# A decoder layer whose dense products are multiplied by Strassen's algorithm instead of block by block

## The chip, the cores and the metric

The kernel runs on one core of one Trainium2 chip. The metric is the device time of one execution in microseconds (us). The kernel before took 1522.94 us (median of 3 runs, 1522.55 to 1523.62).

## The reference

One layer on 1024 tokens of width 1024, in float32: an RMS norm, one wide projection whose columns feed two branches (a gated MLP with spatial mixing, and a Mamba-2 scan, SSD), their outputs projected and merged, and two more dense products at the end.

```python
h = rms_norm(x, norm_g)
u, v, z_a, z_b, xbc, dt_raw, g_a, g_b = split(h @ w_in)        # 1024 x 10272
o_a = gmlp_branch(u, v, z_a, ...) @ w_oa                       # 1024 x 1024
xbc = silu(causal_depthwise_conv(xbc, conv_w, conv_b))         # xs 2048, B 512, C 512 columns
y   = ssd_scan(xs, softplus(dt_raw + dt_bias), a_log, B, C, d_skip)
o_b = gated_group_rms_norm(y, z_b, ssm_norm_g) @ w_ob          # 2048 x 1024
x   = x + (sigmoid(g_a) * o_a + sigmoid(g_b) * o_b) @ w_out    # 1024 x 1024
x   = x + sigmoid(rms_norm(x, ple_norm_g) @ w_pg) * (p @ w_ple)
return rms_norm(x, final_g)
```

## The kernel before, in words

To keep float32 accuracy, both operands of a product are split into two float32r parts, hi (a rounded copy) and lo (the rest), and three products are summed: hi·hi, hi·lo, lo·hi. `mm3` (L89) issues them; every dense matmul has line L97, but those of v (L515). Splitting costs one copy (ScalarE, L228 or L112) and one subtraction (GpSimd L229 for weights of the projections, VectorE L113, L573 elsewhere).

The normed and transposed h stays on chip as `hhi`, `hlo`, 8 k-tiles by two halves of 512 tokens. `in_proj` (L237) loads 128 columns of `w_in`, splits them and makes 48 matmuls of 512 columns (8 k-tiles, 2 halves, 3 parts) into two PSUM banks. From there each stage reads: `conv_tile` (L332) does the convolution on VectorE straight from PSUM (L339), `ssd_chunk` (L352) is the scan of 128 tokens of one of four groups, `z_tile` and `group_out` gate and norm, `gate_tile` writes the tanh of the gates to DRAM. Phase 2 (gMLP) makes v with 768 matmuls of 256 columns, mixes, and projects z_a and u. Phase 3 multiplies `w_ob`, `w_oa` in six parts of 512 rows, adding into tiles `m`; phase 4 multiplies `w_out` (`px`) and `w_pg` (`ppg`). The small product p·w_ple stands at the very start, while x is loaded.

An automatic scheduler sets the order of instructions on each engine from the written program. Loads are on SP's queue, most loads of intermediate results on POOL's; each queue and each engine works in order.

Of the kernel before, what the change touches and what calls it, by code (L numbers as in the profile page):

```python
# [24 lines left out]
O_U, O_V, O_ZA, O_ZB, O_XS, O_B, O_C, O_DT, O_GA, O_GB = (  # L25
    0, 1024, 2048, 3072, 5120, 7168, 7680, 8192, 8224, 9248)


@with_exitstack
def kernel(  # L30
# [38 lines left out]
    tri = const.tile([P, P], F32, name="tri")  # L69
    nc.gpsimd.memset(tri, 1.0)  # L70
    nc.gpsimd.affine_select(out=tri, in_=tri, pattern=[[1, P]], compare_op=ALU.is_ge,
                            fill=0.0, base=0, channel_multiplier=-1)
    triq = const.tile([P, P], F32, name="triq")
    nc.gpsimd.tensor_scalar(out=triq, in0=tri, scalar1=0.25, scalar2=None, op0=ALU.mult)
    # sel[k, m] = 1 in the last row
    sel = const.tile([P, P], F32, name="sel")
    nc.gpsimd.memset(sel, 1.0)
    nc.gpsimd.affine_select(out=sel, in_=sel, pattern=[[0, P]], compare_op=ALU.is_ge,
                            fill=0.0, base=-(P - 1), channel_multiplier=1)
# [8 lines left out]

    def mm3(pst, ahi, alo, bhi, blo, first, last, hh=(0, 1)):  # L89
        # pst[h] += (ahi + alo)^T (bhi + blo), for each half h of b's columns  # L90
        seq = [(ahi, b, h) for h in hh for b in (bhi, blo)] + [(alo, bhi, h) for h in hh]
        seen = set()
        cnt = {0: 0, 1: 0}
        for a, b, h in seq:
            cnt[h] += 1
            o_ = pst[h] if isinstance(pst, list) else pst[:, h, :]
            nc.tensor.matmul(o_, lhsT=a, rhs=b[h],  # L97
                             start=(first and h not in seen), stop=(last and cnt[h] == 3))
            seen.add(h)

    # ------------------------------------------------------------ p w_ple, kept for the end
    hsl = [slice(0, 512), slice(512, 1024)]

    def two(t):
        return [t[:, hsl[0]], t[:, hsl[1]]]

    def load_rows(name, src, row, a, b):
        # a, b: the destinations of the two parts, as halves
        raw = wp.tile([P, 1024], F32, tag="raw", name=f"raw_{name}")
        nc.sync.dma_start(out=raw, in_=src[row:row + P, :])  # L110
        for h in range(2):
            nc.scalar.copy(out=a[h], in_=raw[:, hsl[h]])  # L112
            tt(out=b[h], in0=raw[:, hsl[h]], in1=a[h].bitcast(F32), op=ALU.subtract)  # L113
        return a, b

    def w_slots(name):
        return (two(wp.tile([P, 1024], F32R, tag="whi", name=f"hi_{name}")),
                two(wp.tile([P, 1024], F32R, tag="wlo", name=f"lo_{name}")))

    def big_slots(name):  # L120
        return (two(big.tile([P, 1024], F32R, tag="big", name=f"hi_{name}")),
                two(big.tile([P, 1024], F32R, tag="big", name=f"lo_{name}")))

    ppd = dram.tile([S, D], F32, name="ppd")
    pts = [big.tile([P, NCH // 2, 256], F32, tag="big", name=f"ptm{i}") for i in range(2)]
    p_v = p.rearrange("(t q) e -> q t e", q=P)
    for i in range(2):
        nc.sync.dma_start(out=pts[i], in_=p_v[:, 4 * i:4 * i + 4, :])
        if i == 0:
            wple = [load_rows(f"wple{k}", w_ple, k * P, *w_slots(f"wple{k}")) for k in range(2)]  # L130
    # ------------------------------------------------------------ phase 0: h = rms_norm(x), transposed
    ss0 = const.tile([P, NCH], F32, name="ss0")
    rstd0 = const.tile([P, NCH], F32, name="rstd0")
    xt = []
    for t in range(NCH):
        xv = big.tile([P, D], F32, tag="big", name=f"x0_{t}")
        nc.sync.dma_start(out=xv, in_=x[t * P:(t + 1) * P, :])
        xt.append(xv)

    # per-column vectors, as columns  # L140
    n_cv = 4 * 24
    vrow2 = t2.tile([72, P], F32, tag="hst", name="vrow2")
    o = 0
    offs = {}
    for nm, ap_, n in (("ng", norm_g, 8), ("sg", ssm_norm_g, 16), ("cb", conv_b, 24),
                       ("lg", ln_a_g, 8), ("lb", ln_a_b, 8)):
        nc.scalar.dma_start(out=vrow2[o:o + n, :], in_=ap_.rearrange("(t q) -> t q", q=P))
        offs[nm] = o
        o += n
# [12 lines left out]

    phi = [two(big.tile([P, S], F32R, tag="big", name=f"phi{k}")) for k in range(2)]
    plo = [two(big.tile([P, S], F32R, tag="big", name=f"plo{k}")) for k in range(2)]
    for i in range(2):
        for k in range(2):
            pt = ps_ss(f"ptp{k}_{i}")
            for c in range(4):
                nc.tensor.transpose(out=pt[:, c * P:(c + 1) * P], in_=pts[i][:, c, k * P:(k + 1) * P],
                                    identity=ident)  # L170
            nc.vector.tensor_copy(out=phi[k][i], in_=pt)
            tt(out=plo[k][i], in0=pt, in1=phi[k][i].bitcast(F32), op=ALU.subtract)
# [5 lines left out]
    def halves(dt, tag, name):  # L178
        return [hp_.tile([P, 512], dt, tag=tag, name=f"{name}_{h}") for h in range(2)]

    hhi = [halves(F32R, "hA", f"hhi{k}") for k in range(KD)]
    hlo = [halves(F32R, "hB", f"hlo{k}") for k in range(KD)]
    for hf in range(2):
        h4 = slice(4 * hf, 4 * hf + 4)
        for t in range(4 * hf, 4 * hf + 4):
            junk = t4.tile([P, D], F32, tag="t4", name=f"sq0_{t}")
            act(junk, xt[t], AF.Square, accum_out=ss0[:, t:t + 1])
        rms_rstd(rstd0[:, h4], ss0[:, h4], eps1, 1.0 / D)
        for t in range(4 * hf, 4 * hf + 4):
            ts(out=xt[t], in0=xt[t], scalar1=rstd0[:, t:t + 1], scalar2=None, op0=ALU.mult)  # L190
        if hf == 0:
            pv = ps_ss("pv")
            nc.tensor.transpose(out=pv[:, 128:128 + NV2], in_=vrow2[:NV2, :], identity=ident[:NV2, :NV2])
            nc.tensor.transpose(out=pv[:, 0:n_cv], in_=vrow1, identity=ident[:n_cv, :n_cv])
            nc.vector.tensor_copy(out=vT, in_=pv[:, 128:128 + NV2])
            nc.vector.tensor_copy(out=cwT, in_=pv[:, 0:n_cv])
        for k in range(KD):
            pt = ps_ss(f"pt0_{hf}_{k}")
            for i in range(4):
                nc.tensor.transpose(out=pt[:, i * P:(i + 1) * P],  # L200
                                    in_=xt[4 * hf + i][:, k * P:(k + 1) * P], identity=ident)
# [150 lines left out]
    def ssd_chunk(g, c, xs, bT, cT, hst):  # L352
# [63 lines left out]
        if last:  # L416
            return None
# [309 lines left out]
```

## Time and profile before

| | |
|---|---|
| median of 3 runs | 1522.94 us |
| span of the profiled execution | 1521.2 us (1.7 us under the median) |
| TensorE (PE) busy | 1495.8 us, 98% |
| VectorE (DVE), ScalarE (ACT), GpSimd (POOL) busy | 694.6, 582.8, 524.2 us |
| bytes moved by DMA | 163.62 MB, mean 108 GB/s |

The span runs from the first to the last instruction. The chain of work that ended last is followed back from the end; what stands on it sets the time. A busy share of another engine matters only where TensorE waits for it.

### The profile page before, as it was taken

How to read it: one execution, taken by the hardware profiler on the slowest of the kernel's cores; microseconds unless marked ns; L12 is line 12 of the kernel's file. 1: busy time of each engine (PE TensorE's matmuls, PEld its weight loads, DVE VectorE, ACT ScalarE, POOL GpSimd, SP SyncE). 2: the span in 40 equal slices, each digit the busy share in tenths (PEclk: the TensorE clock that was granted, in tenths of full speed). 3: DMA queues.
4: the chain of work that ended last, by engine and by line, in shares of the span. 5: the costliest groups of instructions: out<-in, count | busy, mean ns of one | idle time of the engine just before them, and what ended most of it. 6: DMA issues, size and time to landing. Idle time of an engine off the chain costs nothing.

```text
span 1521.2 us, 18888 instructions
## 1 busy us (share of the span) xinstructions
PE 1495.8 (98%) x7628; PEld 1248.1 (82%) x7628; DVE 694.6 (46%) x1012; ACT 582.8 (38%) x924; POOL 524.2 (34%) x446
## 2 busy tenths in 40 slices
PE   6999999999999999999999999999999999999997
PEld 5788888878888888889999988888888888888885
DVE  5554477557656764430000432333133567831554
ACT  6453565555556545442112211122322111421454
POOL 1223656465557645651222211222322233100110
PEclk9999999999999999999999999999999999999999
DMA  8321222322142232342221221223332345534541
GB/s 277 104 73 56 84 70 64 117 83 70 56 125 76 64 112 83 117 152 71 84 83 56 77 77 56 69 85 116 125 111 97 135 170 186 189 125 150 215 186 56
DMA packets 124763, 163.62 MB, mean 108 GB/s; under 512 B 6292, under 2 KB 97636, under 8 KB 124676
## 3 DMA queue, kind: packets, MB, share of 16 engines
q1 hardware_dynamic: 107984, 102.90, 21.4%
q0 software_dynamic: 16464, 59.43, 11.4%
q8 instruction: 60, 0.98, 0.3%
q14 instruction: 27, 0.22, 0.0%
q10 hardware_dynamic: 228, 0.08, 0.0%
HBM read 128.71 MB, written 33.69 MB: 107 GB/s over the span
## 4 chain that ended last, share of the span: by engine, by line
PE 92%; issue 2%; DVE 2%; ACT 1%; DMA 1%; POOL 1%; SPq 0%; DVEq 0%; ACTq 0%; POOLq 0%
PE po L97 16%; PE ps_xs L97 11%; PE ps_zb L97 9%; PE psv L515 6%; PE ps_ga L97 6%; PE ps_za L97 6%; PE ps_gb L97 6%; PE px L97 6%; PE ps_u L97 6%; PE ppg L97 5%; PE ps_C L97 3%; PE ps_B L97 2%; PE pyo L406 2%; PE pyd L401 2%; PE psv L544 1%
## 5 line engine op out<-in xcount | busy, mean ns | idle before, releaser
L97 PE MATMUL po<-yh,whi_o 128*128 128x512 f32 x384 | 149.5, 389 | 0.5 <-DVE gt L603 0.5
L97 PE MATMUL po<-yl,whi_o 128*128 128x512 f32 x384 | 149.4, 389 | 0.0
L97 PE MATMUL po<-yh,wlo_o 128*128 128x512 f32 x384 | 118.2, 389 | 0.0
L97 PE MATMUL ps_zb<-hhi,whi_zb 128*128 128x512 f32 x256 | 101.9, 398 | 0.0
L97 PE MATMUL ps_zb<-hlo,whi_zb 128*128 128x512 f32 x256 | 101.3, 396 | 0.0
L97 PE MATMUL ps_xs<-hhi,whi_xs 128*128 128x512 f32 x256 | 100.4, 392 | 0.0
L97 PE MATMUL ps_xs<-hlo,whi_xs 128*128 128x512 f32 x256 | 100.0, 391 | 0.0
L229 POOL TENSOR_TENSOR wlo_o<-raw_o,whi_o 128x1024 fp32r<-128x1024 f32 x24 | 57.8, 2407 | 103.5 <-ACT whi_o L228 103.5
L97 PEld LDWEIGHTS po<-yh,whi_o 128*128 128x128 f32 x384 | 72.1, 188 | 15.9 <-issue 0.9
L97 PEld LDWEIGHTS po<-yh,wlo_o 128*128 128x128 f32 x384 | 72.1, 188 | 14.9
L97 PEld LDWEIGHTS po<-yl,whi_o 128*128 128x128 f32 x384 | 72.0, 188 | 14.9
L414 POOL TENSOR_TENSOR cv_xs<-cv_xs,ex 128x128 f32<-128x128 f32 x112 | 72.3, 672 | 34.1 <-DVE ex L409 34.0
L394 ACT ACTIVATE lm<-lm,cs 128x128 f32<-128x128 f32 x256 | 78.6, 389 | 12.3 <-DMA lm<-csd 11.8
L339 DVE SCALAR_TENSOR_TENSOR cv_xs<-ps_xs,cwT,cv_xs 128x1023 f32<-128x1023 f32 (+2 forms) x48 | 61.5, 1281 | 43.0 <-ACT cv_xs L336 42.0
L97 PE MATMUL ps_zb<-hhi,wlo_zb 128*128 128x512 f32 x256 | 80.7, 394 | 0.0
L97 PE MATMUL ps_xs<-hhi,wlo_xs 128*128 128x512 f32 x256 | 79.8, 393 | 0.0
L528 DVE BATCH_NORM_STATS2 bst<-v 128x6 f32<-128x128 f32 x64 | 13.2, 278 | 141.2 <-ACT v L518 141.2
L228 ACT CAST whi_o<-raw_o 128x1024 fp32r<-128x1024 f32 x24 | 25.3, 1052 | 133.7 <-PE po L97 99.9
L515 PE MATMUL psv<-whi_v,hhi 128*128 128x256 f32 x256 | 72.9, 285 | 0.0
L392 ACT ACTIVATE ex<-lm 64x512 f32<-64x512 f32 x56 | 35.3, 631 | 97.8 <-DMA lm<-csd 82.8
L515 PE MATMUL psv<-whi_v,hlo 128*128 128x256 f32 x256 | 72.4, 283 | 0.0
L515 PE MATMUL psv<-wlo_v,hhi 128*128 128x256 f32 x256 | 72.4, 283 | 0.0
(289 smaller groups left out, 3833.6 us busy)
## 6 DMA issues: line engine op xcount, KB each, us to landing
lm<-csd POOLq DMA_DIRECT2D x32, 512.0 KB, 4.3
raw_xs<-in_w_in_dram SPq DMA_DIRECT2D x16, 512.0 KB, 4.6
raw_zb<-in_w_in_dram SPq DMA_DIRECT2D x16, 512.0 KB, 3.8
ybd<-cv_xs SPq DMA_DIRECT2D x16, 512.0 KB, 5.2
yraw<-ybd POOLq DMA_DIRECT2D x16, 512.0 KB, 3.8
raw_o<-in_w_ob_dram SPq DMA_DIRECT2D x16, 512.0 KB, 3.4
gt<-tad POOLq DMA_DIRECT2D x16, 512.0 KB, 4.3
x<-in_x_dram SPq DMA_DIRECT2D x8, 512.0 KB, 8.7
```

The lines of the kernel that those rows point to most:

```text
L97: nc.tensor.matmul(o_, lhsT=a, rhs=b[h], start=(first and h not in seen), stop=(last and cnt[h] == 3))
L228: nc.scalar.copy(out=whi[:, :n], in_=raw[:, :n])
L229: nc.gpsimd.tensor_tensor(out=wlo[:, :n], in0=raw[:, :n], in1=whi[:, :n].bitcast(F32), op=ALU.subtract)
L339: stt(out=a[:, sh:], in0=ps[:, :S - sh], scalar=cw(k, ci), in1=a[:, sh:], op0=ALU.mult, op1=ALU.add)
L392: act(ex[h * HD:(h + 1) * HD], lv[h * HD:(h + 1) * HD, :, h, :], AF.Exp)
L394: act(lm[:, r_, :], lm[:, r_, :], AF.Relu, bias=cs[:, c, g * HG + r_:g * HG + r_ + 1], scale=-1.0)
L401: nc.tensor.matmul(pyd[h * HD:(h + 1) * HD, (r_ // 2) * P:(r_ // 2 + 1) * P], lhsT=xdt[:, r_, :], rhs=lm[:, r_, :], start=True, stop=True)
L406: nc.tensor.matmul(pyo[:, j * P:(j + 1) * P], lhsT=hst[:, 2 * j:2 * j + 2, :].rearrange("s r d -> s (r d)"), rhs=cT[:, cl], start=True, st ...
L414: nc.gpsimd.tensor_tensor(out=xs[j][:, cl], in0=xs[j][:, cl], in1=ex[:, j, :], op=ALU.add)
L515: nc.tensor.matmul(pf[:, i, :], lhsT=a[hf][:, i * P:(i + 1) * P], rhs=w_[:, k % 4, :], start=(k == 0 and n_ == 0), stop=(k == KD - 1 and n ...
L528: nc.vector.bn_stats(out=bst[:, c, j, :], in_=v[j][:, c, :])
L544: nc.tensor.matmul(psv[:, i * P:(i + 1) * P], lhsT=v[j][:, 4 * hf + i, :], rhs=wsT[:, g, :], start=True, stop=True)
```

## The change

All dense products but dt's (1024 x 1024 times 1024 x 32) and p·w_ple become multiplications of one form, `gemm`: the left operand gives 256 columns (two tiles of 128), the right operand is 1024 x 1024; both are cut in half along the inner dimension too, so there are 2 x 2 blocks on each side and four result blocks of 128 x 512. Strassen's algorithm in Winograd's form needs seven block products (of 4 k-tiles by 3 parts, 12 matmuls) where the plain way has eight. There are 60 such multiplications, of 84 matmuls of 512 columns.

- The left side (`a_side`): four additions on VectorE make S1 to S4, and seven pieces are split (ACT copy, POOL subtraction, L146), for each multiplication. Buffers: three raw tiles (a multiplication takes two), four hi and four lo pieces of seven.
- The right side: seven combinations (B11, B21, B22, T1 to T4) of 4 k-tiles, split, 56 tiles that stay on chip. For h they are made at the start (`h_sums`). For the five later products (two halves of `w_ob`, `w_oa`, `w_out`, `w_pg`) `sums_b` forms them early and writes them to DRAM, and `load_b` reads and splits them into the same 56 slots (8 more for one combination), each free when the last multiplication of the product before has used it.
- Between products PSUM is copied out three times (`snap`, ACT), and each result block is the sum of a bank and a copy (`mat`, VectorE).
- Since results come as halves of two tiles, stages meet through DRAM: conv's output `xbd`, the scan's `yd`, gated `ybd`, v, sums of the output products `md`. Loads and stores go to SP's queue. The scan's three products a chunk with xs are one instruction each now (POOL L622, L630, VectorE L631); convolution reads a float32 tile on chip (L494, L497), no longer PSUM. p·w_ple moves between `w_oa` and `w_out`.
- Order: convolution and v first, then the 32 scan chunks spread over 20 multiplications, then gMLP and gates, then the output products.

```diff
-    def in_proj(name, col):
-        whi, wlo = w_cols(name, col)
-        ps = ps_mm(f"ps_{name}")
-        for k in range(KD):
-            mm3(ps, whi[:, k, :], wlo[:, k, :], hhi[k], hlo[k], k == 0, k == KD - 1)
-        return flat(ps)
...
+        def split(nm, raw, lo_on):
+            hi = wpl.tile([P, 4, P], F32R, tag="wh", name=f"{nm}h_{name}", bufs=4)
+            lo = wpl.tile([P, 4, P], F32R, tag="wl", name=f"{nm}l_{name}", bufs=4)
+            nc.scalar.copy(out=hi, in_=raw)
+            lo_on(out=lo, in0=raw, in1=hi.bitcast(F32), op=ALU.subtract)
+            return hi, lo
+        res = {}
+        res["B11"] = split("a11", a11, ptt)
+        res["B21"] = split("a12", a12, ptt)
+        s1 = sm("s1")
+        tt(out=s1, in0=a21, in1=a22, op=ALU.add)
+        s2 = sm("s2")
+        tt(out=s2, in0=s1, in1=a11, op=ALU.subtract)
+        res["T2"] = split("s2", s2, ptt)
+        res["T1"] = split("s1", s1, ptt)
...
+    def gemm(name, loads, B, epi):
+        A = a_side(name, loads)
+        def prod(pst, c, first):
+            for k in range(4):
+                mm3(pst, (A[c][0][:, k, :], A[c][1][:, k, :]), B[c][k], first and k == 0, k == 3, True)
...
+        xb = ps_mm(f"x_{name}")
+        prod(xb, "B11", True)
+        u1 = snap("u1", xb)
+        ab = ps_mm(f"a_{name}")
+        prod(ab, "B21", True)
+        epi(0, 0, ab, u1)
+        prod(xb, "T2", False)
+        u2 = snap("u2", xb)
+        cb = ps_mm(f"c_{name}")
+        prod(cb, "T1", True)
+        prod(xb, "T3", False)
+        u3 = snap("u3", xb)
+        epi(1, 1, cb, u3)
+        db = ps_mm(f"d_{name}")
+        prod(db, "T4", True)
+        epi(1, 0, db, u3)
+        prod(cb, "B22", False)
+        epi(0, 1, cb, u2)
...
+                dma(out=t, in_=src)
+                res[c].append(split_b(f"{nm}_{c}_{k}", t, ("ap", "av", "vp", "av")[k], c == "B22"))
```

In `split_b` the first letter names the engine of the copy (a: ACT, v: DVE), the second that of the subtraction (v: DVE, p: POOL).

Three places of the order on the engines. First POOL inside the scan of group 0, before: one chunk and the start of the next (`wlo_xs`: lo part of the next convolution's weights, 1024 columns; `hst`, `dx`, `dxl`: the scan's state; `cv_xs`: its output).

```order
L414 TENSOR_TENSOR cv_xs_0_787<-cv_xs_0_787,ex_4_1262 128x128
L414 TENSOR_TENSOR cv_xs_1_850<-cv_xs_1_850,ex_4_1262 128x128
L414 TENSOR_TENSOR cv_xs_2_913<-cv_xs_2_913,ex_4_1262 128x128
L414 TENSOR_TENSOR cv_xs_3_976<-cv_xs_3_976,ex_4_1262 128x128
L229 TENSOR_TENSOR wlo_xs_1_1911<-raw_xs_1_1909,whi_xs_1_1910 128x1024
L427 TENSOR_TENSOR hst_5_1369<-hst_4_1302,cdec 128x512
L379 TENSOR_TENSOR dx_5_1323<-xdt_5_1321,dec_502 128x512
L386 TENSOR_TENSOR dxl_5_1326<-dx_5_1323,dxh_5_1325 128x512
```

The same engine in the scan of group 0 now (`a11l` to `s4l`: lo parts of the left pieces of two multiplications, `cv_1` and the next; `xin`: the scan's output).

```order
L622 TENSOR_TENSOR xin_6_3100<-xin_6_3100,dcol 128x512
L598 TENSOR_TENSOR dx_6_3120<-xdt_6_3118,dec_477 128x512
L146 TENSOR_TENSOR a11l_cv_1_3733<-raw_cv_1_3728,a11h_cv_1_3732 128x512
L146 TENSOR_TENSOR a12l_cv_1_3737<-raw_cv_1_3730,a12h_cv_1_3736 128x512
L603 TENSOR_TENSOR dxl_6_3124<-dx_6_3120,dxh_6_3122 128x512
L146 TENSOR_TENSOR s2l_cv_1_3745<-s_cv_1_3742,s2h_cv_1_3744 128x512
L146 TENSOR_TENSOR s1l_cv_1_3749<-s_cv_1_3740,s1h_cv_1_3748 128x512
L577 DMA lm_0_3368<-csd 128x1024
L630 TENSOR_TENSOR xin_6_3100<-xin_6_3100,ex_6_3126 128x512
L146 TENSOR_TENSOR s3l_cv_1_3755<-s_cv_1_3752,s3h_cv_1_3754 128x512
L622 TENSOR_TENSOR xin_7_3165<-xin_7_3165,dcol 128x512
L146 TENSOR_TENSOR a22l_cv_1_3759<-raw_cv_1_3730,a22h_cv_1_3758 128x512
```

Between two chunks there stood one or no split of weights; now there are six, and the chunk's own work has one more instruction.

The same stretch on VectorE now (`cva`: a half tile of the convolution; `s_cv`: the sums S1 to S4 of the left side; `cv`: a result block, PSUM bank plus copy).

```order
L501 SCALAR_TENSOR_TENSOR cva_3558<-cvt_3563,cva_3558 128x512
L497 SCALAR_TENSOR_TENSOR cva_3567<-cv_0_1_3542,cwT,cva_3567 128x512
L631 TENSOR_TENSOR xin_6_3100<-pyd_6_3139,xin_6_3100 128x512
L482 TENSOR_TENSOR cv_0_0_3490<-c_cv_0_3515,u_cv_0_3513 128x512
L497 SCALAR_TENSOR_TENSOR cva_3567<-cv_0_1_3542,cwT,cva_3567 128x512
L154 TENSOR_TENSOR s_cv_2_3983<-s_cv_2_3981,raw_cv_2_3969 128x512
L497 SCALAR_TENSOR_TENSOR cva_3567<-cv_0_1_3542,cwT,cva_3567 128x512
L582 TENSOR_TENSOR cbm_7_3171<-pbc_7_3169,triq 128x128
```

The convolution's taps (L497) read two operands on chip, where before one of the two (L339) was in PSUM.

Third, POOL where the right side goes over from the first half of `w_ob` (o0) to the second (o1); with numbers (`lo_yb1`: lo parts of the new right side, `a11l_o1` and the like: of the left side).

```order
L118 TENSOR_TENSOR lo_yb1_T3_0_10922<-ldb_yb1_T3_0_10919,hi_yb1_T3_0_10921 128x512
L146 TENSOR_TENSOR a11l_o1_0_10996<-raw0_o1_0_10991,a11h_o1_0_10995 128x512
L118 TENSOR_TENSOR lo_yb1_T3_2_10934<-ldb_yb1_T3_2_10931,hi_yb1_T3_2_10933 128x512
L146 TENSOR_TENSOR a12l_o1_0_11000<-raw1_o1_0_10993,a12h_o1_0_10999 128x512
L118 TENSOR_TENSOR lo_yb1_T4_0_10946<-ldb_yb1_T4_0_10943,hi_yb1_T4_0_10945 128x512
L118 TENSOR_TENSOR lo_yb1_T4_2_10958<-ldb_yb1_T4_2_10955,hi_yb1_T4_2_10957 128x512
L146 TENSOR_TENSOR s2l_o1_0_11008<-s2_o1_0_11005,s2h_o1_0_11007 128x512
L146 TENSOR_TENSOR s1l_o1_0_11012<-s1_o1_0_11003,s1h_o1_0_11011 128x512
```

Before, POOL split weights alone here (24 instructions of 1024 columns in all of phase 3), and VectorE split the right side (L573).

## Rows read from the trace of the kernel before

**Rows 1.** The page: busy time, share and instructions by engine.
```profile
PE 1495.8 (98%) x7628; PEld 1248.1 (82%) x7628; DVE 694.6 (46%) x1012; ACT 582.8 (38%) x924; POOL 524.2 (34%) x446
```
**Rows 2.** The page: the chain that ended last, shares by engine.
```profile
PE 92%; issue 2%; DVE 2%; ACT 1%; DMA 1%; POOL 1%; SPq 0%; DVEq 0%; ACTq 0%; POOLq 0%
```
**Rows 3.** The chain in order of time: start us, us, what, matmuls.
```profile
789.45 23.03 PE psv L515 x192
...
904.43 10.90 PE ps_za L97 x48
```
**Rows 4.** Stretches: busy us and instructions by engine, clock, DMA share, GB/s.
```profile
0.00:13.00 13.00, 1.94 (x8) 1.57 (x8) 3.60 (x6) 3.79 (x6) 3.88 (x17) 1.00 0.82 238
13.00:16.00 3.00, 2.98 (x11) 2.76 (x12) 1.83 (x4) 1.38 (x3) 0.00 (x0) 1.00 1.04 413
480.00:520.00 40.00, 40.00 (x228) 32.83 (x227) 28.15 (x38) 23.81 (x45) 21.59 (x22) 1.00 0.24 76
720.00:760.00 40.00, 40.00 (x250) 36.24 (x249) 3.29 (x16) 8.11 (x10) 9.55 (x4) 1.00 0.26 79
```
**Rows 5.** Single lines: instructions, ns min/median/max, times, forms.
```profile
L396 DVE TENSOR_TENSOR lm<-lm,cbm x32: 1216/1336/4800, 107.0 to 635.7; 128x1024 f32<-128x1024 f32 x32
...
L601 DVE SCALAR_TENSOR_TENSOR m<-gt,m x16: 677/685/2471, 1204.8 to 1245.3; 128x512 f32<-128x512 f32 x16
...
L596 DVE TENSOR_TENSOR m<-m,po x48: 678/681/689, 1116.6 to 1242.3; 128x512 f32<-128x512 f32 x48
...
L536 DVE TENSOR_SCALAR v<-v,mv,rsv x64: 329/335/2499, 861.3 to 879.9; 128x128 f32<-128x128 f32 x64
...
L386 POOL TENSOR_TENSOR dxl<-dx,dxh x28: 1265/1282/1298, 140.2 to 633.0; 128x512 fp32r<-128x512 f32 x28
...
L379 POOL TENSOR_TENSOR dx<-xdt,dec x28: 1036/1046/2024, 138.4 to 630.5; 128x512 f32<-128x512 f32 x28
```
**Rows 6.** VectorE in time, two places: start us, us, instruction.
```profile
196.51 4.80 DVE L396 TENSOR_TENSOR lm<-lm,cbm 128x1024 f32<-128x1024 f32 x1
...
1242.89 2.47 DVE L601 SCALAR_TENSOR_TENSOR m<-gt,m 128x512 f32<-128x512 f32 x1
```
**Rows 7.** POOL in time, the same two places.
```profile
196.84 2.39 POOL L229 TENSOR_TENSOR wlo_xs<-raw_xs,whi_xs 128x1024 fp32r<-128x1024 f32 x1
199.19 1.04 POOL L427 TENSOR_TENSOR hst<-hst,cdec 128x512 f32<-128x512 f32 x1
...
1242.41 2.39 POOL L229 TENSOR_TENSOR wlo_o<-raw_o,whi_o 128x1024 fp32r<-128x1024 f32 x1 [1.72 <-ACT whi_o L228]
```
**Rows 8.** Groups by line, ACT: out<-in xcount, busy us, mean ns, idle before.
```profile
L112 ACT CAST hi_wo<-raw_wo 128x512 fp32r<-128x512 f32 x16 | 9.2, 618 | 9.3 <-DMA raw_wo<-in_w_out_dram 7.4 <-PE po L97 1.8
L594 ACT COPY m<-po 128x512 f32<-128x512 f32 x16 | 8.6, 587 | 11.4 <-PE po L97 11.4
```
**Rows 9.** The page: DMA by queue (q1 is SP's, q0 POOL's): packets, MB, share.
```profile
q1 hardware_dynamic: 107984, 102.90, 21.4%
q0 software_dynamic: 16464, 59.43, 11.4%
```
**Rows 10.** PE in time, in the head: start us, us, instruction.
```profile
15.64 0.63 PE L97 MATMUL pple<-hi_wple,phi 128*128 128x512 f32 x1
16.07 0.63 PE L97 MATMUL pple<-lo_wple,phi 128*128 128x512 f32 x1
...
17.28 0.40 PE L97 MATMUL pple<-hi_wple,phi 128*128 128x512 f32 x1
17.52 0.40 PE L97 MATMUL pple<-lo_wple,phi 128*128 128x512 f32 x1
```
**Rows 11.** Who waited for whom, PE: us in total, times, longest.
```profile
PE ptp L169 <- DMA ptm<-in_p_dram: 11.1, 2, 6.3
```
**Rows 12.** Stretches at the end, columns as in rows 4.
```profile
1507.00:1515.00 8.00, 3.77 (x17) 2.81 (x15) 4.33 (x8) 5.60 (x10) 0.00 (x0) 1.00 0.17 66
1515.00:1521.00 6.00, 0.00 (x0) 0.00 (x0) 1.58 (x3) 1.27 (x2) 0.00 (x0) 0.55 0.23 87
```

More of the change, by code (lines that the diff above doesn't have):

```diff
@@ L87 @@
     nc.gpsimd.memset(eps4, 4.0 * EPS)
[L89 to L99, printed above, removed]
@@ L102 @@
[L102 to L118, printed above, removed]
@@ L120, in big_slots @@
[L120 to L143, printed above, removed]
-    offs = {}
[L145 to L149, printed above, removed]
@@ L161, in cw @@
         return cwT[:, k * 24 + i:k * 24 + i + 1]
[L163 to L172, printed above, removed]
     def rms_rstd(dst, ssum, eps, scale):
@@ L247 @@
[L247 to L257 removed]
+    more = []
@@ new lines, in h_slot, with split_b @@
+    def h_slot(name, own=False):
+        if own and more:
+            return more[-1].tile([P, HALF], F32R, tag="H1", name=name, bufs=8)
+        return hpl.tile([P, HALF], F32R, tag="H", name=name)
+    def split_b(name, raw, how, own=False):
+        hi, lo = h_slot(f"hi_{name}", own), h_slot(f"lo_{name}", own)
+        if how[0] == "a":
+            nc.scalar.copy(out=hi, in_=raw)
+        else:
+            nc.vector.tensor_copy(out=hi, in_=raw)
+        (tt if how[1] == "v" else ptt)(out=lo, in0=raw, in1=hi.bitcast(F32), op=ALU.subtract)
+        return hi, lo
@@ new lines, with e_tile, ld_tile, cv_tile @@
+    ep = ctx.enter_context(tc.tile_pool(name="ep", bufs=1, reuse_waits="tile"))
+    pools = {}
+    def e_tile(name):
+        return ep.tile([P, HALF], F32, tag="e", name=name, bufs=4)
+    def ld_tile(name):
+        p_, n_ = pools["ld"]
+        return p_.tile([P, HALF], F32, tag="ld", name=name, bufs=n_)
+    def cv_tile(name):
+        return pools["cv"].tile([P, S], F32, tag="cv", name=name, bufs=2)
+    def mat(name, src, add):
+        t = e_tile(name)
+        if add is None:
+            nc.scalar.copy(out=t, in_=src)
+        else:
+            tt(out=t, in0=src, in1=add, op=ALU.add)
+        return t
@@ new lines, in ssd_chunk, with v_pair, epi @@
+        hsts[g] = hn
+    def v_pair(m):
+        def epi(i, j, src, add):
+            if add is not None:
+                src = mat(f"v{m}{i}{j}", src, add)
+            t = e_tile(f"vg{m}{i}{j}")
+            act(t, src, AF.Gelu_apprx_tanh)
+            jj = 2 * m + i
+            pt = ps_ss(f"pv{m}{i}{j}")
+            for c in range(4):
+                nc.tensor.transpose(out=pt[:, c * P:(c + 1) * P], in_=t[:, c * P:(c + 1) * P],
+                                    identity=ident)
+            for c in range(4):
+                nc.vector.bn_stats(out=bst[:, 4 * j + c, jj, :], in_=pt[:, c * P:(c + 1) * P])
+            o_ = e_tile(f"vt{m}{i}{j}")
+            nc.scalar.copy(out=o_, in_=pt)
+            dma(out=vd.rearrange("c q d -> q c d")[:, 4 * j:4 * j + 4, jj * P:(jj + 1) * P],
+                in_=o_.rearrange("q (c d) -> q c d", d=P))
+        c = O_V + 2 * m * P
+        gemm(f"v{m}", w_loads(w_in_k, c, c + P), B, epi)
@@ new lines @@
+    rms_rstd(mv[:, :, 1], mv[:, :, 1], eps1, 1.0)
+    gates = [lambda m=m: gate_pair(O_GA, tad, m) for m in range(4)] + \
+            [lambda m=m: gate_pair(O_GB, tbd, m) for m in range(4)]
+    with tc.tile_pool(name="ssd", bufs=1, reuse_waits="tile") as sp:
+        for g in range(G):
+            units = []
+            if g + 1 < G:
+                units += [lambda m=m: conv_pair(g + 1, m) for m in range(3)]
+            if g > 0:
+                units += [lambda m=m: z_pair(g - 1, m) for m in range(2)]
+            take = (2, 0, 0, 3)[g]
+            units += gates[:take]
+            gates = gates[take:]
+            n, c = len(units), 0
+            for u, unit in enumerate(units):
+                while c < (u + 1) * NCH // n:
+                    ssd_chunk(sp, g, c)
+                    c += 1
+                unit()
@@ new lines, with o_stage, epi @@
+    pa.__exit__(None, None, None)
+    def o_stage(nm, w, row, part, get):
+        Bn = load_b(nm, get)
+        wk = w[row:row + 1024, :].rearrange("(k q) c -> q k c", q=P)
+        for m in range(4):
+            def epi(i, j, src, add):
+                n = f"{part}{m}{i}{j}"
+                r0 = (2 * m + i) * P
+                piece = lambda d: d[r0:r0 + P, hsl[j]]
+                c = mat(f"o{n}", src, add)
+                if part > 0:
+                    g_ = ld_tile(f"og{n}")
+                    dma(out=g_, in_=(tbd if part == 1 else tad)[2 * m + i, :, hsl[j]])
+                    pm = ld_tile(f"om{n}")
+                    dma(out=pm, in_=piece(md[part - 1]))
+                if part == 1:
+                    ptt(out=c, in0=c, in1=pm, op=ALU.add)
+                    stt(out=c, in0=g_, scalar=1.0, in1=c, op0=ALU.add, op1=ALU.mult)
+                elif part == 2:
+                    stt(out=c, in0=g_, scalar=1.0, in1=c, op0=ALU.add, op1=ALU.mult)
+                    ptt(out=c, in0=c, in1=pm, op=ALU.add)
+                dma(out=piece(md[part]), in_=c)
+            gemm(f"o{part}_{m}", w_loads(wk, 2 * m * P, (2 * m + 1) * P), Bn, epi)
```

1064 lines of the change are left out of this document (622 added, 442 removed).

## The prediction

> **What bounds the kernel now.** Read the page's busy time first: TensorE is busy 1495.8 us of a span of 1521.2, every other engine under half of it [rows 1]. Busy alone could hide gaps, so the chain that ended last comes next: 92% of it is matmuls [rows 2]. Then the waits of TensorE: the only long one is for the first DMA, 11.1 us in all [rows 11], and at the end some 8 us remain after the last matmul [rows 12]. So the kernel is bound by matmul issue, and the price of a matmul is read from the chain: 48 of 512 columns in 10.90 us are 0.227 us each, 192 of 256 columns in 23.03 us are 0.120 [rows 3].
>
> A second resource shows in single lines. L396, a VectorE product of two tiles on chip, takes 1216 ns at best and 4800 at worst; L601, half as wide, 677 and 2471; L596, which reads one operand from PSUM, never more than 689 [rows 5]. The two timelines say why. The VectorE instruction that began at 196.51 ended at 201.31, 1.08 us after POOL's second one had ended (199.19 + 1.04); the one at 1242.89 ended at 1245.36, 0.56 after POOL's [rows 6, 7]. So VectorE with two operands on chip and POOL do not run together: each holds a path that both need until its instruction is done. POOL waits too (L379: 1046 at the median, 2024 at most) [rows 5]. I call it the pair. What an instruction holds of it, from these ends: VectorE 0.55 us for 512 columns, 1.08 for 1024; POOL 1.28 less some 0.12 of start that overlaps, 1.16 (L386), or 0.92 with a broadcast operand (L379). Before, nobody suffers: POOL 34%, and TensorE stays at 40.00 of 40 us even in the scan [rows 1, 4].
>
> **The change, part by part.** *Matmuls.* Before: 5472 of 512 columns, 1242 us, and 768 for v, 92; together 1334, which leaves 162 of the busy time for scan, transposes and the rest. Now 60 multiplications of 84, plus 96 for p·w_ple: 5136 x 0.227 = 1166, and 64 transposes for v, some 6 us. TensorE's work falls by 162 us, to 1334.
>
> *Copies on ACT.* Seven splits and three copies out of PSUM a multiplication, 10 x 0.6 = 6 us of its 19.1 [rows 8]; two splits of 1024 columns, 2.1, go. ACT's sum rises to some 920 us, about 410 of them in the scan's 507 (below). Hidden, if nothing else delays it.
>
> *The pair.* POOL: 7 subtractions x 60 = 420 for left sides, 86 for right sides, 140 for the scan, 108 others: 754 instructions, 861 us held. VectorE: 4 sums x 60 = 240, 86 right-side subtractions, 192 convolution taps and gates (formerly fed from PSUM), 32 scan products of 1024 columns, 336 others: 886 with two operands on chip, some 494 us, and 138 with one, some 33 us. Together 1388 us that cannot overlap, more than the 1334 of TensorE. The old sum, 316 POOL and 393 VectorE instructions, is about 650.
>
> Of the one-operand instructions the trace shows only L536, 329 ns at best and 2499 at worst, so it waits as well [rows 5]. The 52 new copies from chip to chip on VectorE have no row; they hold nothing if they behave like L596 and 0.27 us each if like L536, so 0 to 14 us; I take 14. The Trainium skill ("VectorE: DVE Perf Modes", section "Mode 2×_2P — use both read ports for one tensor") says that such a float32 copy spreads one tensor over both read ports; by it the pair's sum is 1388, and without it 1374.
>
> *Where it matters.* Taking the program in its new order, TensorE against the pair, us: head (to the last combination of h) 35 and 62; convolution of group 0 and v 140 and 128; the 19 multiplications among the scan 473 and 507; gMLP and gates 272 and 265; three output products with p·w_ple 253 and 261; the last two 161 and 166. The larger of each: 62 + 140 + 507 + 272 + 261 + 166 = 1408. Add about 12 until the first x has landed (the old head: 13 us with little work [rows 4]) and 9 at the end [rows 12]: 1429.
>
> Taken stretch by stretch, one multiplication each, the larger of the resources sum to 1515, with the same 21 to 1536. The 107 between are excess that buffers would have to carry into a neighbouring stretch. 51 of it stands where one right side gives way to the next: 28 splits (14 on POOL, 14 on VectorE, 7 of those with a copy) have to happen within two multiplications, while their slots come free product by product; at the last hand-over to `w_oa` the pair has 56 us of work in 36 of matmuls. That cannot move, so I leave it in full. Of the other 56, mostly in the scan, the four buffered pieces of seven can carry much; I leave 20. So 1429 + 51 + 20 = **1500**, against a profiled 1521; with the 1.7 us by which the median exceeds the span, 1502.
>
> *Costed at nothing.* SP issues 846 DMAs instead of 205 and moves some 266 MB for 103; with POOL's queue 311 MB for 162 [rows 9]. At 0.37 us of issue that is 313 us of SP's time, under the matmuls. The rate is 166 GB/s in the scan and about 270 from gMLP on; the head shows 413 with every DMA engine busy [rows 4]. Only the hand-over into the first output product asks for more, 17 MB in 45 us. If that cover goes, a load comes late by some 5 us there, up to 25 us in all.
>
> **Rivals.** *The pair carries its excess nowhere (slower).* POOL is in order: a subtraction for the left side stands behind a scan instruction that waits for VectorE, which waits for POOL. Then every stretch pays its larger resource, 1536, and the late transfers above, 25: about 1560. It decides as soon as matmuls wait for a `lo` piece in most multiplications of the scan. For it: 507 us of the pair against 473 of TensorE in the scan, with ACT at 410. Against it: before, the scan lost nothing.
>
> *TensorE stays the bound (faster still).* If buffers carry all but the hand-overs' shortest part, each section costs its larger: 1429 to 1450. For it: the sections' sums lie close to TensorE's. Against it: a path used at 95%.
>
> *The clock.* At the start matmuls stand 0.43 us apart (15.64, 16.07) after TensorE had waited, then 0.24 (17.28, 17.52): the lower level, 1.2 GHz, though the clock's column has 1.00 there [rows 4, 10]; at the end, idle, the mean is 0.55 [rows 12]. If waits in the scan brought that level back for a third of its 473 us, it would add some 150: 1650. The Trainium skill ("TensorE: Matmul & The Clock Gate", Part 1) says that the throttled state is the default and that activity releases it; by that rule a TensorE fed in pieces could fall back again and again. The old trace has 1.00 between head and end, and no gaps to try the rule on.
>
> **How the numbers follow.** A measurement of this kernel tells 0.2% (3 us) from no change. The forecast (1455 to 1519) has 0.38; TensorE as the bound (below 1455) 0.15; a sum within 3 us of the old by chance 0.06; the pair unrelieved (1526 to 1600) 0.36; the clock, above 1600, 0.05. Faster 0.53, same 0.06, slower 0.41. The range leaves out less than a tenth at the low end and the clock at the high end: 1420 to 1600. The forecast's own range is 1455 to 1519.
>
> **What would show it.** Right: about 5136 dense matmuls 0.227 apart; TensorE busy under 92% of the span; POOL busy some 1000 us; two-operand VectorE lines with a mean far above 0.69 us; TensorE's waits led by POOL's `lo` pieces in the scan and by right-side splits at five places. Wrong: TensorE above 95% busy (the pair did not bind), VectorE's two-operand lines at 0.69 (no pair), waits led by DMA (transfers bind), or a clock well under 1.00.

## The result, and the profile after

The changed kernel took 1746.81 us (median of 4 runs, 1745.54 to 1750.39), the kernel before 1523.22: a ratio of 1.147 (95% interval 1.145 to 1.149). The forecast was 1502, the range ended at 1600: slower where faster was the likelier, and outside the range. Times here and below are medians of fast runs; a single slow one, of `f2_swap` (2055.20 us), is left out.

The page of the changed kernel, which answers to [rows 1], with the slices of VectorE, POOL and the granted clock:

```profile
PE 1458.7 (84%) x6596; PEld 1149.5 (66%) x6596; DVE 1332.7 (76%) x1575; ACT 860.1 (49%) x1636; POOL 1148.8 (66%) x852
...
DVE  6888558988997499957558999864868985476886
...
POOL 4644666677679377858865546766879997475632
PEclk9698999999999799988999999998999999988898
```

TensorE stands idle for 286 us instead of 25, and no other engine is full. Its busy time fell by 37 us, not by 162: some 45 of the 125 us between are matmuls at the lower clock (last section), the rest was not taken apart. VectorE is busy 1333 us and POOL 1149; the same instructions at their undisturbed durations (0.68 us for 512 columns on VectorE, 1.28 on POOL, [rows 5]) would take by estimate some 980 each. The difference, about 350 and 170 us, I put down to standing for the path: in `e4_pair` below a VectorE instruction of 0.68 us takes 1.74 beside POOL, with nothing else to wait for.

The stretches in the order of the program (columns as in [rows 4]), cut where the prediction's sections meet: head, convolution and v, scan, gMLP and gates, three output products, last two:

```profile
20.00:91.00 71.00, 46.05 (x166) 31.60 (x166) 60.53 (x64) 26.21 (x47) 47.41 (x35) 0.76 0.13 32
91.00:246.00 155.00, 131.21 (x568) 103.65 (x568) 111.08 (x169) 63.83 (x110) 82.58 (x67) 0.96 0.49 159
246.00:877.00 631.00, 534.94 (x2691) 421.68 (x2690) 510.26 (x588) 380.27 (x762) 451.04 (x332) 0.94 0.46 143
877.00:1212.00 335.00, 290.13 (x1307) 233.80 (x1305) 259.30 (x332) 130.23 (x233) 199.76 (x165) 0.96 0.66 218
1212.00:1511.00 299.00, 268.99 (x1120) 213.01 (x1120) 218.33 (x197) 115.72 (x205) 250.27 (x166) 0.95 0.73 238
1511.00:1744.00 233.00, 183.90 (x736) 143.00 (x736) 168.77 (x212) 129.72 (x247) 116.05 (x78) 0.89 0.61 195
```

Against the larger of TensorE and pair (with the 12 us of the start and 9 of the end, 74, 140, 507, 272, 261, 175), the sections took 91, 155, 631, 335, 299 and 233. Every one is over, by 315 us together; the prediction allowed 71.

Groups by line (out<-in, count | busy us, mean ns of one | idle before), which answer to [rows 5]:

```profile
L497 DVE SCALAR_TENSOR_TENSOR cva<-cv,cwT,cva 128x512 f32<-128x512 f32 x72 | 86.0, 1195 | 1.0
L613 DVE TENSOR_TENSOR lm<-lm,cbm 128x1024 f32<-128x1024 f32 x32 | 55.3, 1728 | 25.9 <-ACT lm L612 25.9
L528 DVE SCALAR_TENSOR_TENSOR zt<-zt,z 128x512 f32<-128x512 f32 x32 | 39.5, 1238 | 3.4 <-ACT zt L527 3.1
...
L631 DVE TENSOR_TENSOR xin<-pyd,xin 128x512 f32<-128x512 f32 x32 | 21.9, 683 | 13.4 <-POOL xin L630 13.4
```

L631, with one operand in PSUM, still takes 683 ns. The two-operand lines take 1.1 to 1.7 us: the pair binds as forecast. But TensorE's waits (us in total, times, longest) are led by VectorE, not by POOL's lo pieces: added up by the engine that ended them, 166 us end with VectorE, 63 with ACT, 38 with POOL, 8 with a DMA. The longest, against [rows 11]:

```profile
PE pyd L618 <- DVE lm L613: 42.4, 13, 8.7
PE pth L950 <- DVE hn L946: 16.6, 6, 5.1
PE c_cv L125 <- DVE hi_t L117: 14.8, 1, 14.8
PE pt L270 <- DVE x L266: 9.2, 3, 7.6
PE pbc L584 <- DVE cbm L582: 9.2, 10, 2.2
```

By product, TensorE is idle 37 us before the first matmul of T1's product (15 of them one wait for the right side, in the head) and 16 before T4's (each needs a fresh PSUM bank), 28 before B22's (it adds into a bank that VectorE's `mat` must have read), 20 at the first product of a multiplication, and 68 in the scan's own matmuls. (The expectation of `f1_banks62` below has 39 and 19 for T1 and T4, from a rougher count.)

### The profile page after: what moved, and what is told of

Same layout as the page of the kernel before. It is cut to its first block, busy times and chain, and to the rows that moved or that the text cites. A ratio compares the mean times of both kernels' runs of the same rounds, so it can differ in the third digit from the quotient of the medians.

```text
span 1744.3 us, 20817 instructions
## 1 busy us (share of the span) xinstructions
PE 1458.7 (84%) x6596; PEld 1149.5 (66%) x6596; DVE 1332.7 (76%) x1575; ACT 860.1 (49%) x1636; POOL 1148.8 (66%) x852
## 5 line engine op out<-in xcount | busy, mean ns | idle before, releaser
L497 DVE SCALAR_TENSOR_TENSOR cva<-cv,cwT,cva 128x512 f32<-128x512 f32 x72 | 86.0, 1195 | 1.0
L494 DVE SCALAR_TENSOR_TENSOR cva<-cv,cwT,cva 128x511 f32<-128x511 f32 (+2 forms) x72 | 78.8, 1094 | 6.0 <-ACT cva L490 5.5
L618 PE MATMUL pyd<-lm,xdt 128*64 128x128 f32 x512 | 41.1, 311 | 46.7 <-DVE lm L613 42.4
L613 DVE TENSOR_TENSOR lm<-lm,cbm 128x1024 f32<-128x1024 f32 x32 | 55.3, 1728 | 25.9 <-ACT lm L612 25.9
L630 POOL TENSOR_TENSOR xin<-xin,ex 128x512 f32<-128x512 f32 x28 | 37.5, 1338 | 41.9 <-DVE ex L629 41.8
L501 DVE SCALAR_TENSOR_TENSOR cva<-cvt,cva 128x512 f32<-128x512 f32 x48 | 52.5, 1094 | 14.2 <-ACT cvt L500 13.5
L603 POOL TENSOR_TENSOR dxl<-dx,dxh 128x512 fp32r<-128x512 f32 x28 | 46.5, 1661 | 12.1 <-ACT dxh L601 12.0
L622 POOL TENSOR_TENSOR xin<-xin,dcol 128x512 f32<-128x512 f32 x32 | 41.6, 1300 | 13.8 <-PE pxt L592 13.8
L490 ACT ACTIVATE cva<-cv,vT,cwT 128x512 f32<-128x512 f32 x48 | 38.6, 803 | 12.6 <-DVE cv L482 12.6
L528 DVE SCALAR_TENSOR_TENSOR zt<-zt,z 128x512 f32<-128x512 f32 x32 | 39.5, 1238 | 3.4 <-ACT zt L527 3.1
L626 PE MATMUL pyo<-xin,hst 128*128 128x128 f32 x224 | 39.2, 329 | 0.0
L146 POOL TENSOR_TENSOR a11l_cv<-raw_cv,a11h_cv 128x512 fp32r<-128x512 f32 x12 | 18.0, 1497 | 30.3 <-ACT a11h_cv L145 30.2
```

The source lines that it names most:

```text
L490: act(a, r[:, hsl[h]], AF.Identity, scale=cw(3, ci), bias=vec("cb", ci))
L494: stt(out=a[:, sh:], in0=r[:, :HALF - sh], scalar=cw(k, ci), in1=a[:, sh:], op0=ALU.mult, op1=ALU.add)
L497: stt(out=a, in0=r[:, HALF - sh:S - sh], scalar=cw(k, ci), in1=a, op0=ALU.mult, op1=ALU.add)
L501: stt(out=a, in0=th, scalar=1.0, in1=a, op0=ALU.add, op1=ALU.mult)
L528: stt(out=th, in0=th, scalar=1.0, in1=src, op0=ALU.add, op1=ALU.mult)
L603: ptt(out=dxl, in0=dxf, in1=dxh.bitcast(F32), op=ALU.subtract)
```

## Experiments

**The price of the pair by itself.** No layer; independent instructions of 512 columns. `gate()` makes each step wait for the one before. The steps in short:

```python
pool(30); gate()              # POOL alone
two(30); gate()               # VectorE, both operands on chip, alone
pool(30); two(60); gate()
pool(30); fromps(60); gate()  # VectorE, one operand in PSUM
pool(30); copy(60); gate()    # VectorE, chip to chip, one operand
pool(30); actc(60); gate()    # ACT copies
# last step, 30 times: one POOL; VectorE from PSUM, on chip, from PSUM
```

> The price of the pair by itself, no layer computed: in this order 30 POOL subtractions of 512 columns alone; 30 VectorE subtractions with both operands on chip alone; 30 POOL beside 60 of these; 30 POOL beside 60 VectorE additions with one operand in PSUM; 30 POOL beside 60 VectorE copies from chip to chip; 30 POOL beside 60 ACT copies; 30 POOL beside 90 of VectorE, two PSUM to one on chip. Prices of the prediction: 38, 20, 30 x (1.16 + 0.55) + 30 x 0.68 = 72, then 41 (no hold), 38 to 46, 38, and 30 x (0.55 + 2 x 0.68) = 57 or more. If the pair costs more than the holds that I took: over 80 in the third, and the PSUM form slower than 0.69 in the fourth.

Stretches of this kernel, one for each step (third and last step: while POOL runs). Columns: us, then DVE, ACT, POOL busy (instructions), clock, DMA:

```profile
7.60:44.40 36.80, 0.07 (x1) 0.00 (x0) 36.64 (x30) 1.00 0.00 0
45.00:63.20 18.20, 18.20 (x31) 0.00 (x0) 0.00 (x0) 1.00 0.00 0
63.90:114.10 50.20, 50.20 (x31) 0.00 (x0) 50.03 (x30) 1.00 0.00 0
132.90:169.50 36.60, 36.60 (x61) 0.00 (x0) 36.51 (x30) 1.00 0.00 0
170.30:222.70 52.40, 52.37 (x63) 0.00 (x0) 41.97 (x30) 1.00 0.00 0
223.50:260.50 37.00, 0.04 (x2) 31.26 (x60) 36.79 (x30) 1.00 0.00 0
261.20:311.20 50.00, 50.00 (x60) 0.00 (x0) 49.76 (x30) 1.00 0.00 0
```

One POOL and one VectorE instruction take 50.0 / 30 = 1.67 us together; the prediction's holds give 1.16 + 0.55 = 1.71. The Trainium skill ("SBUF — State Buffer", section "Terms", shared port pair) calls it an exclusive lock held for the whole instruction; the trace agrees but for 0.15 us (alone the two take 1.22 and 0.60, 1.82 in sum). The PSUM form costs POOL nothing (36.5). Copies from chip to chip cost it (41.97 - 36.64) / 30 = 0.18 us, with one copy beside each POOL instruction; I had taken 0.27 for each copy. In the last step the scheduler set one PSUM-fed instruction beside each pair of POOL and on-chip VectorE, and the other 30 behind. The 30 beside hide completely (50.0 us in all, as in the third step): with nothing to wait for but the path, the path is used without a gap. **The prices were right.**

**Undoing the algorithm, keeping the order.**

```diff
+        for i in range(2):
+            for j in range(2):
+                ps = ps_mm(f"c{i}{j}_{name}")
+                for h in range(2):
+                    a, b = A[f"A{i + 1}{h + 1}"], B[f"B{h + 1}{j + 1}"]
+                    ...
+                epi(i, j, ps, None)
```

> The changed kernel with the plain eight block products in place of Strassen's seven: no sums S1 to S4, four splits of the left side instead of seven, four blocks of the right side instead of seven combinations, no copies of PSUM between products; order, half tiles and the way through DRAM stay. TensorE gets 60 x 12 x 0.227 = 163 us more, some 1497 in all; the pair some 970 instead of 1388. Queues (VectorE and POOL hold each other up in order, and TensorE waits for what Strassen adds to both): 1540 to 1600, TensorE over 93% busy, clock at 0.98 or more. Reordering (the loss comes from half tiles, DRAM and the new order, not from the additions): above 1680, TensorE waiting as now.

1606.03 us (ratio 1.055, 1.053 to 1.056), between the two cases. The page:

```profile
PE 1519.5 (95%) x7308; PEld 1241.9 (77%) x7308; DVE 699.9 (44%) x990; ACT 688.3 (43%) x1319; POOL 693.9 (43%) x558
```

So the new order (half tiles, the way through DRAM) costs 1606 - 1523 = 83 us by itself: TensorE is idle 85 us of the span instead of 25, and busy 24 us longer. Which of the two, half tiles or DRAM, was not separated. Strassen's form on top of it takes 163 us of matmuls away and makes the kernel 141 slower: its additions, splits and waits cost some 304.

**Is TensorE the limit?** One of the three matmuls of each block product is left out (hi of the left times lo of the right).

```diff
-        seq = ((a[0], b[0]), (a[0], b[1]), (a[1], b[0]))
+        seq = ((a[0], b[0]), (a[1], b[0]))
```

> The changed kernel with one of the three matmuls of every block product left out (hi times lo): 1712 matmuls of 512 columns fewer, 389 us less for TensorE (945 left); all splits, sums, copies and loads stay. If VectorE, POOL and ACT with their order set the time by themselves (queues alone): 1600 to 1720. If TensorE's work and its waits add up, since neither is hidden behind the other: 1350 to 1450. If the pair is full as soon as TensorE is out of the way: down to 1409 (1388 and 21), no lower.

1739.49 us (ratio 1.144, 1.141 to 1.146): 389 us of matmuls are worth 7.

```profile
PE 1161.2 (67%) x4884; PEld 877.9 (51%) x4884; DVE 1361.7 (78%) x1575; ACT 855.6 (49%) x1632; POOL 1161.7 (67%) x852
...
ACT hi_yb_B L115 <- DMA ldb_yb_B<-cb_yb_u: 78.7, 4, 75.1
PE x_o L125 <- ACT hi_yb_B L115: 78.2, 2, 77.5
```

That is 19 us above the highest case expected. The scan's stretch did not get shorter (first to last scan product 637 us, 623 with all matmuls). One wait is new (the two last lines, from the list of waits), 77.5 us for the right side of the first output product, whose sums come late through DRAM; without it the cut would have given at most 85 of 389. **Outside that wait VectorE, POOL and ACT, in their order, set the time by themselves.** The granted clock fell to 0.833 here and TensorE is idle for 575 us of the span; the time stayed.

**Relieving the path or VectorE.** Left side's subtractions left out, hi standing for lo; then all on VectorE; then, with these, the sums S1 to S4 on POOL; then, each against the changed kernel, the sums left out and the convolution's taps left out (of several like edits the first is shown):

```diff
-            lo_on(out=lo, in0=raw, in1=hi.bitcast(F32), op=ALU.subtract)
-            return hi, lo
+            return hi, hi
```

> The 420 subtractions of the left side left out; hi stands for lo in the matmuls, which stay 5136. The pair falls by 487 us to about 900; TensorE's work is unchanged. Queues or path: 1450 to 1560, clock back to 0.98 or more, two-operand lines of VectorE down to 0.7 to 0.9 us. Clock or buffers as the cause by themselves (TensorE falls to the lower level at every hand-over, four pieces of seven are too few): above 1650 with a clock as low as now.

```diff
-        res["B11"] = split("a11", a11, ptt)
+        res["B11"] = split("a11", a11, tt)
...
```

> All 420 subtractions of the left side on VectorE instead of POOL; nothing else. By the prices of the prediction the pair falls by 420 x (1.16 - 0.55) = 256 us to 1132, and VectorE's own work rises from some 977 to 1262. Path (the time in which both hold the shared path is what counts): about 1560 to 1620. Queues (VectorE's order is what TensorE waits for, and it gets longer by 285 us of own work but loses the waits for POOL): 1650 to 1750. Buffers or clock alone: within 20 us of 1747.

```diff
-        tt(out=s1, in0=a21, in1=a22, op=ALU.add)
+        ptt(out=s1, in0=a21, in1=a22, op=ALU.add)
...
```

> e2_lo_dve (subtractions of the left side on VectorE) with the 240 sums S1 to S4 on POOL in exchange; the computation is complete. Against e2_lo_dve (1685) the pair's sum rises by 240 x (1.16 - 0.55) = 146 us to 1278, VectorE's own work falls by 163 to about 1100. If the shared path counts: slower than e2_lo_dve, 1720 or more. If VectorE's own queue counts: faster than e2_lo_dve, 1600 to 1660.

```diff
-        res["T2"] = split("s2", s2, ptt)
+        res["T2"] = split("s2", a11, ptt)
...
```

> The 240 sums S1 to S4 left out; plain quarters of the weights are split in their place. VectorE's own work falls by 163 us, the pair's by 132. Leaving out POOL's 487 us of holds gave 162, a third of them. If a microsecond of VectorE counts like one of the path: about 1703. If VectorE's queue is what TensorE waits for: 1650 or below.

```diff
-                for k in (2, 1, 0):
-                    ...
```

> The 144 taps of the convolution left out (three of four; the SiLU and the rest stay). VectorE's own work falls by 98 us, the pair's by 80, nearly all within the first 900 us. By the sums S (77 us for 163): about 1700. If the chain from the taps through ACT's tanh (ACT waits 121 us there) is what holds the scan up: 1650 or below.

| left out or moved | VectorE's own work | pair | time | gain |
|---|---|---|---|---|
| subtractions left out | 0 | -487 | 1584.49 (1.040, 1.036 to 1.043) | 162 |
| subtractions on VectorE | +285 | -256 | 1685.21 (1.106, 1.103 to 1.109) | 62 |
| the same, sums on POOL | +122 | -110 | 1710.09 (1.122, 1.118 to 1.125) | 37 |
| sums left out | -163 | -132 | 1669.34 (1.096, 1.093 to 1.099) | 77 |
| taps left out | -98 | -80 | 1676.91 (1.102, 1.100 to 1.104) | 70 |

Only the second met one of its cases (queues); 1584, 1669 and 1677 lie between their two, 1710 lies 10 us under that of the path. None gives back what it takes off: a microsecond of the path held by POOL is worth 0.33, one of VectorE's own work 0.47 (sums) to 0.71 (taps). Sums and taps hold the path too, so by the path the same gains are 0.58 and 0.88, and the two causes are not separated there. Exchanging sums for subtractions between the engines lost some 25 us against `e2_lo_dve`, with 163 us less on VectorE and 146 more on the path: both seem to count, neither alone is the bound. TensorE's first wait in `e3_no_lo` is still VectorE's mask `lm` (24.5 us).

**Both reliefs, and both with the smaller TensorE.**

> e3_no_lo and g1_two_thirds together: the left side's 420 subtractions left out (hi stands for lo) and one of three matmuls left out. With a third less for TensorE alone the time stayed at 1739, so that is what VectorE, POOL and ACT need among themselves at 1388 us of the pair. If that time goes down by as much as the path is relieved: 1739 - 487 = 1252, and e3_no_lo's 1584 was then TensorE with its waits. If VectorE, POOL and ACT wait for each other whatever the path carries: about 1577, as in e3_no_lo.

1459.29 us (0.959, 0.957 to 0.961), between the two cases: with TensorE out of the way the same 487 us of the path are worth 280 instead of 162.

> e1_plain8 (eight products) with one of three matmuls left out: TensorE 1497 - 1952 x 0.227 = 1054, the pair some 970. If the vector engines' time follows the path one to one: 1739 - 418 = 1321, so that in e1_plain8 TensorE hides it. If the new order's chain (DRAM, scan, epilogues) holds it up by itself: 1500 or more.

1361.07 us (0.895, 0.893 to 0.897), near the first case: the plain form in the new order was bound by TensorE in the main, whose 443 us less gave back 245.

> Both of the left side's costs left out, the sums S1 to S4 and the 420 subtractions; the 5136 matmuls stay. Pair 769 us, VectorE's own work about 814, TensorE 1334. If what remains is TensorE and the new order's own 84 us (as e1_plain8 had over the kernel before): 1429 - 62 + 84, some 1440 to 1460, TensorE at 93% or more. If the two reliefs only add (162 and 77): 1508, TensorE waiting still.

1528.22 us (1.003, 1.002 to 1.004): 219 us less, not even the 239 of the two reliefs apart. The page:

```profile
PE 1388.6 (91%) x6596; PEld 1118.0 (73%) x6596; DVE 868.6 (57%) x1335; ACT 856.9 (56%) x1636; POOL 504.4 (33%) x432
```

Even with the left side's sums and subtractions free, the seven products are no faster than the kernel before: 138 us of idle TensorE remain, among them 26 before T1's product and 16 before B22's. The path's holds, 769 us, are then half of the span, so a full path is not what is left.

**Room and order.** Six PSUM banks for products and two for the scan; 16 KB a partition freed by leaving T3 out (control), then used for a second buffer of each scan tile, or for seven left pieces and six epilogue tiles; the plain form with all the room:

> Six PSUM banks for the products and two for the scan instead of five and three. TensorE now stands idle 39 us before the first matmul of T1's product and 19 before T4's, the two that need a fresh bank in the middle of a multiplication. If banks are what keeps TensorE from working ahead: 30 to 60 us faster (1690 to 1717) where no scan runs, perhaps given back by the scan. If the epilogues on VectorE are late by more than a bank can cover: within 15 us of 1747.

1788.28 us (1.174, 1.172 to 1.177), 41 slower, in neither case: the scan takes 44 us longer (668 against 623, first to last product), the rest as long as before. TensorE's idle time before T1's product did fall, from 37 to 19 us, but this bought nothing. That the scan would gain from more than three banks was not tried in this form.

```diff
-    hpl = ctx.enter_context(tc.tile_pool(name="hpool", bufs=56))
+    hpl = ctx.enter_context(tc.tile_pool(name="hpool", bufs=48))
...
+            B["T3"] = B["T2"]
```

> A control that gives back 16 KB a partition: T3 is not formed or split, T2's tiles stand in for it (56 slots of the right side become 48); the matmuls stay. It leaves out 4 splits at each of 6 right sides, some 20 us of the pair: by what the pair was worth so far (a third) 5 to 30 us faster than 1747, so 1717 to 1742.

> The control h1_t3 with two buffers instead of one for cbm, bh, bl, xdt, dx, dxh, dxl and ex of the scan (the kernel before had two of xdt, ex and cbm). If single buffers make the scan a chain through three queues: 40 to 100 us faster than h1_t3, all in the scan's 622 us. If the queues are late for other reasons: within 15 us of h1_t3.

> The control h1_t3 with seven slots instead of four for hi and for lo of the left side and six instead of four of the epilogue's tiles. If TensorE waits because left sides and epilogues cannot be made ahead: 40 to 120 us faster than h1_t3, in all sections. If the work comes late however many slots there are: within 20 us of h1_t3.

> e1_plain8 (eight products, 1606 us) with the room that Strassen's combinations took: two buffers in the scan as in h2_t3_chunk, eight slots for hi and lo of the left side, eight epilogue tiles, four PSUM banks each for products and scan. If the 84 us between e1_plain8 and the kernel before are the price of the buffers given up: 1515 to 1550. If they are the price of half tiles and of the way through DRAM: above 1585.

Control 1723.33, scan tiles doubled 1706.59 (17 faster, a little over the bound I had set for "no effect", far from 40), left side deeper 1743.06 (20 slower). The plain form with room, four scan banks among it: 1602.97, as without (1606.03). Of these buffers none is what is short.

```diff
-    with _tile.TileContext(nc, schedule_with_timeline_sim=True) as tc:
+    with _tile.TileContext(nc, schedule_with_timeline_sim=False) as tc:
```

> The changed kernel, the same instructions, in another order on every engine: the scheduler orders by readiness and the program as written, without its model of durations. That model knows nothing of the pair, and its order leaves stretches at the end of a group with three to five scan chunks and hardly a multiplication between them. If the order on the queues is a main part of the loss: over 50 us away from 1747 (faster if the model misled it, slower if it helped). If the engines need this time in any order: within 20 us.

```diff
+        yield
         pyd = ps_ss(f"pyd_{n}")
...
-                    ssd_chunk(sp, g, c)
+                    held.append(ssd_chunk(sp, g, c))
+                    next(held[-1])
```

> h2_t3_chunk with the second half of each scan chunk (from the product pyd on) written one multiplication later, so that its mask lm is made well ahead. If TensorE loses by standing behind a chunk's chain in its queue (68 us of idle time before pyd, pbc, pst and pxt): 30 to 70 us faster than h2_t3_chunk's 1707. If the vector engines are late in sum: within 15 us of it.

Another order of the same instructions: 1854.18 us (1.217, 1.215 to 1.219), 107 slower. The deferred half of the scan's chunk: 1702.89 against 1706.59, no change that can be told, as the second case has it. The edit did what it should: between the transposes `pxt` of a chunk and its `pyd` there now stand 36 dense matmuls in the median instead of 22, and TensorE's idle time before `pyd` fell from 28 to 3 us. But that before `pbc` rose from 18 to 40, and the scan's waits sum to 65 us instead of 70: a wait that is taken away comes back at the next product.

## Why the prediction was wrong

- **Right:** 5136 dense matmuls, 0.227 us each where TensorE is fed; the pair and its prices (`e4_pair`); TensorE no longer the bound (`g1_two_thirds`). Transfers, costed at nothing, are hidden from TensorE alone (it waits 8 us for a DMA, at the start): VectorE, for which it waits, itself waits some 68 us for DMAs, 6 before, and what they are worth was not tested.
- **The step that failed** is "the larger of each" per section, with 107 us of excess, of which "the four buffered pieces of seven can carry much; I leave 20". It assumes that the path is kept busy from queues that always hold something ready. Counted by the prices, it is, in one place only, the output products. VectorE's column is third, POOL's fifth; POOL's counts include two and one DMA issues:

```profile
480.00:520.00 40.00, 32.28 (x161) 24.07 (x161) 39.73 (x43) 24.53 (x51) 29.48 (x20) 1.00 0.50 152
1400.00:1440.00 40.00, 36.27 (x148) 28.01 (x147) 33.30 (x27) 15.62 (x28) 39.01 (x26) 0.96 0.75 243
```

In the second, 25 POOL and 19 two-operand instructions hold 25 x 1.16 + 19 x 0.55 = 39 of 40 us. In the first, in the scan, 18 and 26 hold 35, while VectorE is busy 39.73 of 40: its queue is full with standing, and the instructions behind that need nothing of the path, such as `mat` and `xdt`, stand with it. The whole scan averages 33 of 40 by the same count, and the whole program 1388 / 1744 = 80%. In `e4_pair`, where nothing depends on anything, it was 100%. So the sum of holds was a floor, and what had to be added was not 71 but 315. With TensorE out of the way, where the prediction's sum gives 1388 + 21 = 1409, `g1_two_thirds` took 1739, or 1662 without its one new wait. That this is three queues in order, each waiting for the next, is how I read it; the runs show that the order matters (`j2_order`) and that a wait taken away comes back elsewhere (`j1_defer`).
- **The rival on the other side** named this mechanism ("The pair carries its excess nowhere", since "POOL is in order") and gave it 1560. Its sign was right; its size took only the holds stretch by stretch, and its test failed: TensorE's waits end with VectorE (166 us), not with POOL's `lo` pieces (POOL 38 in all).
- **The clock** averaged 0.934, not 1.00. 226 pairs of dense matmuls stand 0.36 to 0.47 us apart instead of 0.227, some 45 us; before, there were 5. They follow waits (below), as the rival said. TensorE's throughput is not what binds, since at 0.833 and a third less work the time was the same; how much the lower level adds through the scan's chain was not separated.
- **The range:** of 0.41 for slower, 0.36 lay below 1600. The order's own cost (83 us, `e1_plain8`) had no term at all, and [rows 4] could give none: before, TensorE was busy 40.00 of 40 us, and no other engine's waits show.

What stays open: why the vector engines need some 270 to 350 us more than the path's holds is not the prices, the buffers that were tried, a sixth bank for the products or TensorE, and it depends on the order of the queues (`j2_order`, 107 us), but no better order was found, so what a good one would save is not known. Late loads and more banks for the scan were not tested by themselves. No version that does the whole computation beat the kernel before; the best was the plain form at 1603.

## What to carry to other kernels

A saving on the bound engine can be worth nothing once the engines that feed it need longer: before trading matmuls for additions, price the additions on the engine and path where they will stand. A sum of exclusive holds is a floor: independent instructions reached it here, work in chains over in-order queues used the path 80% of the time. Test early which side binds, by leaving out a third of the supposed bound's work. Price a reordering by itself: here it cost as much as half the saving.

## What the runs showed of the hardware

After a stand TensorE often goes on at the lower of its two levels, 1.2 GHz. The changed kernel has 34 stretches of three to ten dense matmuls 0.36 to 0.47 us apart; one place in PE's order of time (start us, us, instruction, idle before):

```profile
974.93 0.47 PE L125 MATMUL d_u<-hi_t,a22h_u 128*128 128x512 f32 x1 [3.48 <-DVE za L323]
975.23 0.50 PE L125 MATMUL d_u<-lo_t,a22h_u 128*128 128x512 f32 x1
975.53 0.63 PE L125 MATMUL d_u<-hi_t,a22l_u 128*128 128x512 f32 x1
975.96 0.63 PE L125 MATMUL d_u<-hi_t,a22h_u 128*128 128x512 f32 x1
...
978.88 0.39 PE L125 MATMUL d_u<-lo_t,a22h_u 128*128 128x512 f32 x1
979.11 0.39 PE L125 MATMUL d_u<-hi_t,a22l_u 128*128 128x512 f32 x1
```

After 3.48 us without work they stand 0.30 us apart at first, then 0.43, then 0.23 again; the granted clock is 0.55 from 976.8 to 979.0 and 1.00 from there to 985. The Trainium skill ("TensorE: Matmul & The Clock Gate", Part 1) has the throttled state as the default that activity lifts; these rows agree with that.

A VectorE instruction fed from PSUM fits beside a POOL and an on-chip VectorE subtraction at no cost (1.67 us for the group of three in the last step of `e4_pair`, 1.67 without it). Copies on ACT do not touch the path (POOL 36.79 beside 60 of them, 36.64 alone).
